# Where the low halves of the attention probabilities are formed, and four smaller edits to a hybrid attention and convolution block

## The chip, the cores and the metric

The kernel runs on one core of a Trainium2 chip. Its time is device microseconds of one execution. Three runs of the kernel before gave a median of 634.66 us, between 634.0 and 635.41. A profile is one more execution, recorded by the hardware profiler: this one took 634.12 us, of which 632.3 us lie between the first and the last recorded instruction (the span). The granted TensorE clock was 1.000 in it.

A core has five engines that work through their own instruction streams in order: TensorE (PE in the profile, with its weight loads as PEld), VectorE (DVE), ScalarE (ACT), GpSimd (POOL) and SyncE (SP), which here only issues transfers. They wait for each other through semaphores.

## The reference

One layer of a latent-diffusion backbone: modulated RMS norm, one wide projection, two-dimensional neighbourhood attention that shares its softmax with 256 context keys, a gated short convolution beside it, and an output projection (1024 tokens, width 1024, 8 heads of 64):

```python
h = rmsnorm(x, norm_g) * (1 + scale[:, None]) + shift[:, None]
hc = rmsnorm(ctx, norm_g) * (1 + scale_c) + shift_c
q, k, v, za, u, bg, cg, zc = jnp.split(h @ w_in, SPLIT_POINTS, axis=-1)
...
kc, vc = jnp.split(hc @ w_in[:, D_ATTN:3 * D_ATTN], 2, axis=-1)
...
s = jnp.concatenate([s_lat.reshape(*s_lat.shape[:4], n_lat), s_ctx], axis=-1)
p = jax.nn.softmax(s, axis=-1).astype(v.dtype)
...
attn = neighbourhood_attention(q, k, heads(v), kc, vc, rpb) * jax.nn.silu(za)
conv = gated_short_conv(u, bg, cg, zc, conv_w, conv_b)
x_new = x + gate[:, None] * (jnp.concatenate([attn, conv], axis=-1) @ w_out)
```

`scale` and `shift` come from `silu(c) @ w_ada`, a 1024 x 3072 matrix.

## The kernel before

**Split numbers.** Nearly every product is made of three float32r matmuls: an operand `a` is cast to a high half (`act.copy`, or the exponential itself, written as float32r), the low half is the difference between `a` and that high half (`tensor_tensor(lo, a, hi, subtract)`), and `mm3` adds high times high, high times low and low times high. So each weight or activation tile costs one cast and one difference before TensorE may use it.

**Stages.** (1) From 0 to about 77 us: the slabs of `w_ada`, 1024 x 256 pieces `slabs[m, j]` (m = 0 to 3, j = 0 for shift and 1 for scale), are multiplied by the condition vector (`products`, into the PSUM tile `tr`), `modulation` turns the rows into columns, `transposed` transposes a k-slice of the normed x on TensorE, `turn` applies scale and shift and makes high and low halves, and `first_columns` projects the first 384 columns of the convolution (`acc`). From slab (1, 1) on, slabs are split into halves by `split`, in two parts of four k-tiles (lines 609 to 616). (2) To about 265 us: q, k and v of all heads (`pacc`), norm, rotation, context keys (`cacc`), stored to DRAM. (3) To about 541 us: attention, with the other projections (`pu`) as filler on TensorE. (4) The output projection (`pout`).

**Order.** In stages 1 and 3 the list `strict` is filled: every engine executes its instructions in the order in which the code emits them. In stage 4 it is empty, and a planner orders the instructions of each engine.

**A quarter of the attention.** `quarter(n)` (line 1091) is called 36 times; head and group are `divmod(n, 4)`, a group being 256 of the 1024 queries of a head. Three groups are in work at a time: `n` has its scores made, `e = n - 2` its exponentials, `o = n - 3` its sums with v. In the order of the code:

- TensorE transposes the running maxima `mx` of group `e` into `pmx`; VectorE reduces them to the row maxima `rm` (line 1105).
- `ctx_out(o)`: TensorE multiplies the context exponentials `phc`, `plc` by the context values into `po`.
- `do_dves(3)`: VectorE does waiting chores (weight halves `ul`, convolution `cv`, `cu`, gating `zs`, `tb`), those of the slow queue at most three a quarter; `gating` has more.
- TensorE transposes `rm` back, ScalarE copies it to `mg`; then the latent scores of group `n` (`pss`), the context scores (`pc`, copied to `sc` by ScalarE).
- `ctx_exp(e)` (line 1047): VectorE subtracts `mg` from `sc`, ScalarE makes the exponential twice, as float32r `phc` and in place in `sc`, and GpSimd forms `plc = sc - phc` (line 1055).
- The same for the latent scores: `w` (a view of tile `sb`) minus the maxima, two exponentials, one into `phl`.
- one filler tick (six 512-column matmuls), then `lat_out(o)`: `phl`, `pll` times v.
- VectorE adds the bias to the scores of group `n` (`sb`), and takes maxima into `mx`: `ctx_max` (one operand in PSUM), `lat_max` for two key blocks (both operands in SBUF).
- VectorE forms `pll = w - phl` for group `e` (line 1160).
- the remaining filler ticks; `TICKS[n]` has their number for each quarter, 2 to 4.

Thus the next quarter's first transposes need the last `lat_max`, and its `rm` stands on VectorE behind `pll`.

**The output stage.** `load_wo(wp, nh, f)` loads a 128 x 512 tile of `w_out` into a raw buffer `woraw` through ScalarE's queue, multiplies it by the gate if `nh` is 1, and splits it into `woh` and `wol`; `put_y` does the same for an activation tile. `out_tile` adds the residual and stores. The last tile, (nh, t) = (1, 7), is made in two pieces of 256 columns, each accumulated in its own bank over 24 matmuls, so that the first piece's addition and store run while TensorE makes the second.

Of the kernel before, what the change touches and what calls it, by code (L numbers as in the profile page):

```python
# [10 lines left out]
F32 = mybir.dt.float32  # L11
# [28 lines left out]
def body(tc, es, x, ctxt, w_ada, b_ada, w_in, q_g, k_g, rpbr, w_out, vecs, cst, out):  # L40
# [565 lines left out]
    def norm(xtile, n):  # L606
        dve.tensor_scalar(xtile, xtile, sums[n], None, ALU.mult)

    def split(m, j, part, cast=act.copy):

        if part == 0:
            highs[j] = hcp.tile([P, KT, 256], F32R, name="slabh", tag="AB"[j])
            lows[j] = place(6 + j, [P, KT, 256], F32R, "slabl")
        rows = slice(4 * part, 4 * part + 4)
        cast(highs[j][:, rows], slabs[m, j][:, rows])
        dve.tensor_tensor(lows[j][:, rows], slabs[m, j][:, rows], highs[j][:, rows].bitcast(F32), ALU.subtract)

    def products(m, j, kts=range(KT), parts=(0, 1)):

        if m not in mods:  # L620
            mods[m] = tr()
        rows = mods[m][:4 if m else 2, 256 * j:256 * j + 256]
        split_ = [(c4, highs[j]), (c4, lows[j])] if (m, j) >= (1, 1) else [(c0 if m else c2, slabs[m, j])]
        for i, (c, part) in enumerate(split_):
            for kt in kts if i in parts else ():
                pe.matmul(rows, c[:, kt], part[:, kt], start=(i == 0 and kt == 0 and j == 0),
                          stop=(i == len(split_) - 1 and kt == KT - 1 and j == 1), skip_group_check=True)
# [46 lines left out]
    def transposed(half, k, ts=range(4)):  # L674
        if (half, k) not in pts:
            pts[half, k] = tr()
        for i in ts:
            pe.transpose(pts[half, k][:, i * P:(i + 1) * P], xx[4 * half + i][:, k * P:(k + 1) * P], ident)

    def turn(half, k, on, between=None):  # L680

        modulated(rows_of(hh[k], half), rows_of(hl[k], half),
                  pts.pop((half, k))[:].rearrange("p (r b c) -> p r b c", r=8, b=8), k, 0, on, between)
# [97 lines left out]
        norm(xx[t - 1], t - 1)  # L781
    first_columns(0, 1)
    norm(xx[7], 7)
    split(1, 1, 0)
    split(1, 1, 1, dve.tensor_copy)
    products(1, 0)
    transposed(1, 0)
    turn(1, 0, act)
    load_slab(2, 1)
    load_chunks([4, 5])  # L790
# [113 lines left out]
    def bank(name, tag):  # L904
        return (pss if tag == "S" else psm).tile([P, 512], F32, name=name, tag=tag, bufs=2)
# [60 lines left out]
    class head:  # L966
# [80 lines left out]
        def ctx_exp(self, g):  # L1047
            sc = self.cps[g]
            m = mg[:, g * 256:(g + 1) * 256].rearrange("p (o q) -> p o q", o=1)
            dve.tensor_tensor(sc, sc, m.broadcast_to([P, 2, 256]), ALU.subtract)  # L1050
            ph = ap.tile([P, 2, 256], F32R, name="phc", tag="phc", bufs=2)
            pl = ap.tile([P, 2, 256], F32R, name="plc", tag="plc", bufs=2)
            act.activation(ph, sc, AF.Exp)
            act.activation(sc, sc, AF.Exp)
            pool.tensor_tensor(pl, sc, ph[:].bitcast(F32), ALU.subtract)
            self.cps[g] = ph, pl

        def ctx_out(self, g):
            ph, pl = self.cps.pop(g)
# [31 lines left out]
    def quarter(n):  # L1091

        live = lambda m: 0 <= m < 4 * NH
        ticks = TICKS[n]
        e, o = n - 2, n - 3
        if live(e):
            hd, g = heads[e // 4], e % 4  # L1100
            pm = psm.tile([P, 512], F32, name="pmx", tag="C", bufs=2)
            for i in range(2):
                pe.transpose(pm[:, i * P:(i + 1) * P], mx[:, (2 * g + i) * P:(2 * g + i + 1) * P], ident)
            rm = ap.tile([P, 2], F32, name="rm", tag="rm", bufs=8)
            dve.tensor_reduce(rm, pm[:, :256].rearrange("p (i k) -> p i k", i=2), AX.X, ALU.max)
        if live(o):
            heads[o // 4].ctx_out(o % 4)
        do_dves(3)
        if gating and next(gating[0], "end"):
            gating.pop(0)  # L1110
        if live(e):
            for i in range(2):
                pe.transpose(pm[:, 256 + i * P:256 + (i + 1) * P], rm[:, i:i + 1].broadcast_to([P, P]), ident)
            act.copy(mg[:, g * 256:(g + 1) * 256], pm[:, 256:512])
        now = pair_of(n)
        for i, hd_, j in now:
            hd_.scores(j, sbank[:, i])
        if n == 0:
            next(fill)
            ticks -= 1  # L1120
        if live(n):
            heads[n // 4].ctx_scores(n % 4)
        if live(e):
            hd.ctx_exp(g)
        if e in sbs or e in exps:
            pair, sb = pair_of(e), sbs.pop(e)
            w = both(sb, e, pair)
            dve.tensor_tensor(w, w, maxima_of(e, pair), ALU.subtract)
            exps[e] = [ap.tile([P, 2, 384], F32R, name=m, tag=m, bufs=2) for m in ("phl", "pll")]
            ph, pl = (both(v, e, pair) for v in exps[e])  # L1130
            act.activation(ph, w, AF.Exp)
            act.activation(w, w, AF.Exp)
        for _ in range(n > 0):
            next(fill, None)
        done = []
        if o >= 0:
            pho, plo = exps.pop(o)
            for i, hd_, j in pair_of(o):
                hd_.lat_out(j, pho[:, i], plo[:, i])
                if j in (4, 7):  # L1140
                    done.append((hd_, j // 7))
                    if j == 7 and hd_.s:
                        ready.append(hd_.p)
        if now:
            sb = sbs[n] = sb_new()
            g_ = n % 4
            if g_:
                bt = now[0][1].bt
                bias = bt[:, 1:2].broadcast_to([P, 2, 384]) if g_ == 2 else bt[:, 0:2] if g_ == 1 else bt[:, 1:3]
                dve.tensor_tensor(sb, sbank[:, :, :384], bias, ALU.add)  # L1150
            else:
                for i, hd_, j in now:
                    cols = slice(P, 384) if j == 0 else slice(0, 256)
                    dve.tensor_tensor(sb[:, i, :256], sbank[:, i, :256], hd_.bt[:, 1, cols], ALU.add)
            if live(n):
                heads[n // 4].ctx_max(n % 4)
            for i, hd_, j in now:
                hd_.lat_max(j, sb[:, i])
        if e in sbs or e in exps:
            dve.tensor_tensor(pl, w, ph.bitcast(F32), ALU.subtract)  # L1160
        for _ in range(ticks - (n > 0)):
            next(fill, None)
        for hd_, bank_ in done:
            hd_.finish(bank_)
        do_acts()

    heads = [head(h) for h in range(NH)]
    sbs, exps, ready = {}, {}, []


    def fillers():
# [195 lines left out]
    y, wo = {}, {}  # L1367

    def load_wo(wp, nh, f):
        raw = op.tile([P, 512], F32, name="woraw", tag="woraw", bufs=2)  # L1370
        act.dma_start(raw, w_out[0, f * P:(f + 1) * P, nh * 512:(nh + 1) * 512])
        if nh:
            dve.tensor_tensor(raw, raw, gate[:, 512:], ALU.mult)
        wh = wp.tile([P, 512], F32R, name=f"woh{nh}{f}")
        wl = wp.tile([P, 512], F32R, name=f"wol{nh}{f}")
        act.copy(wh, raw)
        dve.tensor_tensor(wl, raw, wh[:].bitcast(F32), ALU.subtract)  # L1377
        wo[nh, f] = wh, wl
# [38 lines left out]
    def out_tile(ps, nh, t, pieces=(slice(0, 512),)):  # L1417
        rows, cols = slice(t * P, (t + 1) * P), slice(nh * 512, (nh + 1) * 512)
        xr = rp.tile([P, 512], F32, name="xr", tag="xr", bufs=3)
        sp.dma_start(xr, x[0, rows, cols])  # L1420
        ot = rp.tile([P, 512], F32, name="ot", tag="ot", bufs=3)
        if nh:
            for c in pieces:
                part = slice(c.start + 512, c.stop + 512)
                dve.tensor_tensor(ot[:, c], ps[c.start // 256][:, c], xr[:, c], ALU.add)
                sp.dma_start(out[0, rows, part], ot[:, c])
        else:
            dve.tensor_tensor(ot, ps, gate[:, cols], ALU.mult)
            pool.tensor_tensor(ot, ot, xr, ALU.add)
            sp.dma_start(out[0, rows, cols], ot)  # L1430
# [7 lines left out]
    for t in first:  # L1438
        out_tile(first[t], 0, t)
    for n, (nh, t) in enumerate([(0, 6), (0, 7)] + [(1, t) for t in range(NB)]):  # L1440
        pieces = [slice(0, 256), slice(256, 512)] if (nh, t) == (1, NB - 1) else [slice(0, 512)]
        ps = [bank("pout", "USC"[(n + i) % 2 + i]) for i in range(len(pieces))]
        for c, b in zip(pieces, ps):
            for f in FORDER:
                out_mm(b, nh, t, f, c)
        out_tile(ps if nh else ps[0], nh, t, pieces)


# [49 lines left out]
```

## Time and profile before

| | us |
|---|---|
| median of three runs | 634.66 |
| the profiled execution, whole | 634.12 |
| its span | 632.3 |
| ScalarE busy | 327.7 |
| VectorE busy | 447.7 |
| GpSimd busy | 121.4 |
| of which `plc`, 32 subtractions | 42.8 |
| last recorded matmul's start | 629.0 |

A line of the profile names the engine, the operation, the tiles (`out<-in`, buffer numbers left out), the shape of the result and of the input (partitions x elements), the count, and in a summary the busy time and the mean of one in ns. Most instructions of stages 1 to 3 carry the line of a helper, L55, so tiles identify them. In a list in order of time the columns are start and duration in us; a bracket tells how long the engine was idle before the instruction and what ended that. In a list of waits they are the total, the number and the longest. A matmul's recorded duration covers its way through the array, so consecutive matmuls overlap, and only the distances of their starts show the rate: a 512-column matmul is recorded with 0.39 us and followed by the next after 0.23. In a list of stretches the columns after the window are its length and the busy time of PE, PEld, DVE, ACT and POOL with instruction counts, then the clock and the transfers.

### The profile page before, as it was taken

The numbers are of one execution on the slowest core, as the hardware profiler recorded it, in microseconds if no ns is written. First come the engines' busy times: TensorE is split into PE (matmuls) and PEld (weight loads), VectorE is DVE, ScalarE is ACT, GpSimd is POOL, SyncE is SP. The second block draws the span as 40 slices with busy tenths as digits, with TensorE's granted clock in tenths as the row PEclk, the third lists the DMA queues.
The fourth block names the chain that finished last, engine by engine and source line by source line (L and its number), as shares of the span: only waits on it lengthen the run. The fifth ranks groups of instructions, "written<-read, shape, count | busy, mean of one in ns | idle before, by whom it ended". The sixth has DMA issues, their size and how long they took to land.

```text
span 632.3 us, 10096 instructions
## 1 busy us (share of the span) xinstructions
PE 624.3 (99%) x3503; PEld 538.8 (85%) x3504; DVE 447.7 (71%) x834; ACT 327.7 (52%) x705; POOL 121.4 (19%) x134
## 2 busy tenths in 40 slices
PE   8999999999999999999999999999999999999998
PEld 3577899999999999888888888888888888888887
DVE  1887858766856755478898889988998964477411
ACT  5676935424625446345576568567775854352000
POOL 1305014123223222001121111111111112003300
PEclk9999999999999999999999999999999999999999
DMA  8973648867775993975383736683842233965721
GB/s 319 381 268 106 179 116 258 263 195 213 265 245 169 293 337 134 330 221 194 103 286 100 237 104 209 190 277 101 269 131 75 59 103 123 316 204 183 237 101 50
DMA packets 103007, 125.61 MB, mean 199 GB/s; under 512 B 9665, under 2 KB 71577, under 8 KB 101676
## 3 DMA queue, kind: packets, MB, share of 16 engines
q1 hardware_dynamic: 96492, 113.38, 54.8%
q10 hardware_dynamic: 6208, 11.05, 5.6%
q0 software_dynamic: 256, 0.54, 0.4%
q8 instruction: 27, 0.44, 0.3%
q14 instruction: 24, 0.20, 0.1%
HBM read 88.09 MB, written 38.62 MB: 200 GB/s over the span
## 4 chain that ended last, share of the span: by engine, by line
PE 78%; DVE 7%; DMA 6%; issue 6%; ACT 1%; SPq 1%; POOL 1%; DVEq 0%; POOLq 0%; ACTq 0%
PE pu L55 24%; PE pacc L55 21%; PE po L55 7%; PE acc L55 5%; PE cacc L55 4%; PE tr L55 3%; PE pss L55 3%; PE pmx L55 2%; DVE mx L55 2%; PE pout L75 2%; PE pout L76 2%; PE pout L74 2%; PE pc L55 2%; DMA slab<-in_w_ada 2%; DVE sb L55 2%
## 5 line engine op out<-in xcount | busy, mean ns | idle before, releaser
L55 PE MATMUL pu<-h,uh 128*128 128x512 f32 x544 | 169.1, 392 | 0.0
L55 PE MATMUL pacc<-wh,h 128*128 128x384 f32 x512 | 135.1, 338 | 0.0
L55 PEld LDWEIGHTS pu<-h,uh 128*128 128x128 f32 x544 | 98.1, 188 | 17.0
L55 PE MATMUL pu<-h,ul 128*128 128x512 f32 x272 | 106.3, 391 | 0.0
L55 PEld LDWEIGHTS pacc<-wh,h 128*128 128x128 f32 x512 | 92.9, 188 | 0.1
L55 PE MATMUL pacc<-wl,h 128*128 128x384 f32 x256 | 85.6, 335 | 0.0
L55 POOL TENSOR_TENSOR plc<-sc,phc 128x512 fp32r<-128x512 f32 x32 | 42.8, 1339 | 215.9 <-ACT sc L55 159.2
L55 POOL TENSOR_TENSOR ss<-ss,few 128x4 f32<-128x4 f32 (+1 forms) x40 | 41.4, 1038 | 125.3 <-DVE ss L55 125.1
L55 PEld LDWEIGHTS pu<-h,ul 128*128 128x128 f32 x272 | 51.1, 188 | 11.2
L55 DVE TENSOR_TENSOR mx<-mx,sb 128x384 f32<-128x384 f32 (+1 forms) x64 | 59.1, 932 | 2.0
L75 PE MATMUL pout<-wol,yh 128*128 128x512 f32 (+1 forms) x136 | 51.3, 377 | 0.1
L76 PE MATMUL pout<-woh,yl 128*128 128x512 f32 (+1 forms) x136 | 50.7, 377 | 0.0
L74 PE MATMUL pout<-woh,yh 128*128 128x512 f32 (+1 forms) x136 | 49.7, 376 | 0.0
L55 PEld LDWEIGHTS pacc<-wl,h 128*128 128x128 f32 x256 | 48.1, 188 | 0.1
L55 DVE TENSOR_REDUCE ss<-sq 128x4 f32<-128x260 f32 (+1 forms) x40 | 15.7, 394 | 40.8 <-ACT sq L55 40.8
L55 ACT ACTIVATE sq<-pacc 128x256 f32<-128x256 f32 x32 | 12.3, 385 | 52.5 <-PE pacc L55 52.0
L55 ACT COPY mg<-pmx 128x256 f32<-128x256 f32 x32 | 11.9, 373 | 51.7 <-PE pmx L55 45.3
L55 ACT COPY sc<-pc 128x512 f32<-128x512 f32 x32 | 18.8, 589 | 25.8 <-PE pc L55 25.8
L55 ACT ACTIVATE qn<-pacc,ss 128x64 f32<-128x64 f32 x128 | 30.1, 330 | 3.0 <-issue 2.5
L55 DVE TENSOR_TENSOR pll<-sb,phl 128x768 fp32r<-128x768 f32 (+2 forms) x33 | 28.4, 861 | 4.5 <-ACT sb L55 4.5
L55 PE MATMUL po<-phl,v 128*65 128x256 f32 (+2 forms) x160 | 31.2, 291 | 0.0
L75 PEld LDWEIGHTS pout<-wol,yh 128*128 128x128 f32 x136 | 25.6, 188 | 5.2 <-DVE wol L1377 0.5
(163 smaller groups left out, 1266.0 us busy)
## 6 DMA issues: line engine op xcount, KB each, us to landing
uraw<-in_w_in SPq DMA_DIRECT2D x34, 256.0 KB
q_d<-qs SPq DMA_DIRECT2D x32, 256.0 KB
k_s<-k_d SPq DMA_DIRECT2D x8, 1024.0 KB
q_s<-q_d SPq DMA_DIRECT2D x16, 512.0 KB
wr<-in_w_in SPq DMA_DIRECT2D x40, 192.0 KB
slab<-in_w_ada SPq DMA_DIRECT2D x6, 1024.0 KB
v_d<-vs SPq DMA_DIRECT2D x20, 260.0 KB
v<-v_d SPq DMA_DIRECT2D x16, 325.0 KB
```

The source lines that it names most:

```text
L55: i = emit(*a, **kw)
L74: i = pe.matmul(ps, ah, bh, start=first, stop=False)
L75: pe.matmul(ps, ah, bl, start=False, stop=False)
L76: pe.matmul(ps, al, bh, start=False, stop=last)
```

## The change

Five edits in one:

- `ctx_exp` no longer emits the difference `plc`; it returns a function that emits it on VectorE, and `quarter` calls this after the maxima of group `n`.
- The latent difference `pll` is put off: it goes into the list `lat_rest` and is emitted in the next quarter, behind that quarter's `rm`. If the next quarter has two ticks, or there is none, it is emitted at its old place, which is now behind `plc`.
- For slab (1, 1), ScalarE casts the first part and VectorE the second before either difference; the other slabs keep the order cast, difference for each part. TensorE's transposes for `turn(1, 0)` go ahead of the last two k-tiles of `products(1, 0)`.
- The raw tiles of `w_out` get four buffers instead of two.
- The last output tile is cut into 384 and 128 columns, with the banks kept by a piece's first column.

```diff
@@ -606,14 +606,23 @@
     def norm(xtile, n):
         dve.tensor_scalar(xtile, xtile, sums[n], None, ALU.mult)
 
-    def split(m, j, part, cast=act.copy):
+    def cast_slab(m, j, part, cast):
 
         if part == 0:
             highs[j] = hcp.tile([P, KT, 256], F32R, name="slabh", tag="AB"[j])
             lows[j] = place(6 + j, [P, KT, 256], F32R, "slabl")
         rows = slice(4 * part, 4 * part + 4)
         cast(highs[j][:, rows], slabs[m, j][:, rows])
+
+    def rest_of(m, j, part):
+
+        rows = slice(4 * part, 4 * part + 4)
         dve.tensor_tensor(lows[j][:, rows], slabs[m, j][:, rows], highs[j][:, rows].bitcast(F32), ALU.subtract)
+
+    def split(m, j, part):
+
+        cast_slab(m, j, part, act.copy)
+        rest_of(m, j, part)
 
     def products(m, j, kts=range(KT), parts=(0, 1)):
 
@@ -781,10 +790,13 @@
         norm(xx[t - 1], t - 1)
     first_columns(0, 1)
     norm(xx[7], 7)
-    split(1, 1, 0)
-    split(1, 1, 1, dve.tensor_copy)
-    products(1, 0)
+    cast_slab(1, 1, 0, act.copy)
+    cast_slab(1, 1, 1, dve.tensor_copy)
+    rest_of(1, 1, 0)
+    rest_of(1, 1, 1)
+    products(1, 0, range(6))
     transposed(1, 0)
+    products(1, 0, range(6, KT))
     turn(1, 0, act)
     load_slab(2, 1)
     load_chunks([4, 5])
@@ -1052,8 +1064,8 @@
             pl = ap.tile([P, 2, 256], F32R, name="plc", tag="plc", bufs=2)
             act.activation(ph, sc, AF.Exp)
             act.activation(sc, sc, AF.Exp)
-            pool.tensor_tensor(pl, sc, ph[:].bitcast(F32), ALU.subtract)
             self.cps[g] = ph, pl
+            return lambda: dve.tensor_tensor(pl, sc, ph[:].bitcast(F32), ALU.subtract)
 
         def ctx_out(self, g):
             ph, pl = self.cps.pop(g)
@@ -1103,6 +1115,8 @@
                 pe.transpose(pm[:, i * P:(i + 1) * P], mx[:, (2 * g + i) * P:(2 * g + i + 1) * P], ident)
             rm = ap.tile([P, 2], F32, name="rm", tag="rm", bufs=8)
             dve.tensor_reduce(rm, pm[:, :256].rearrange("p (i k) -> p i k", i=2), AX.X, ALU.max)
+        while lat_rest:
+            lat_rest.pop()()
         if live(o):
             heads[o // 4].ctx_out(o % 4)
         do_dves(3)
@@ -1121,7 +1135,7 @@
         if live(n):
             heads[n // 4].ctx_scores(n % 4)
         if live(e):
-            hd.ctx_exp(g)
+            ctx_rest = hd.ctx_exp(g)
         if e in sbs or e in exps:
             pair, sb = pair_of(e), sbs.pop(e)
             w = both(sb, e, pair)
@@ -1156,8 +1170,12 @@
                 heads[n // 4].ctx_max(n % 4)
             for i, hd_, j in now:
                 hd_.lat_max(j, sb[:, i])
+        if live(e):
+            ctx_rest()
         if e in sbs or e in exps:
-            dve.tensor_tensor(pl, w, ph.bitcast(F32), ALU.subtract)
+            lat_rest.append(lambda: dve.tensor_tensor(pl, w, ph.bitcast(F32), ALU.subtract))
+            if n + 1 >= len(TICKS) or TICKS[n + 1] == 2:
+                lat_rest.pop()()
         for _ in range(ticks - (n > 0)):
             next(fill, None)
         for hd_, bank_ in done:
@@ -1165,7 +1183,7 @@
         do_acts()
 
     heads = [head(h) for h in range(NH)]
-    sbs, exps, ready = {}, {}, []
+    sbs, exps, ready, lat_rest = {}, {}, [], []
 
 
     def fillers():
@@ -1367,7 +1385,7 @@
     y, wo = {}, {}
 
     def load_wo(wp, nh, f):
-        raw = op.tile([P, 512], F32, name="woraw", tag="woraw", bufs=2)
+        raw = op.tile([P, 512], F32, name="woraw", tag="woraw", bufs=4)
         act.dma_start(raw, w_out[0, f * P:(f + 1) * P, nh * 512:(nh + 1) * 512])
         if nh:
             dve.tensor_tensor(raw, raw, gate[:, 512:], ALU.mult)
@@ -1422,7 +1440,7 @@
         if nh:
             for c in pieces:
                 part = slice(c.start + 512, c.stop + 512)
-                dve.tensor_tensor(ot[:, c], ps[c.start // 256][:, c], xr[:, c], ALU.add)
+                dve.tensor_tensor(ot[:, c], ps[c.start][:, c], xr[:, c], ALU.add)
                 sp.dma_start(out[0, rows, part], ot[:, c])
         else:
             dve.tensor_tensor(ot, ps, gate[:, cols], ALU.mult)
@@ -1438,11 +1456,11 @@
     for t in first:
         out_tile(first[t], 0, t)
     for n, (nh, t) in enumerate([(0, 6), (0, 7)] + [(1, t) for t in range(NB)]):
-        pieces = [slice(0, 256), slice(256, 512)] if (nh, t) == (1, NB - 1) else [slice(0, 512)]
-        ps = [bank("pout", "USC"[(n + i) % 2 + i]) for i in range(len(pieces))]
-        for c, b in zip(pieces, ps):
+        pieces = [slice(0, 384), slice(384, 512)] if (nh, t) == (1, NB - 1) else [slice(0, 512)]
+        ps = {c.start: bank("pout", "USC"[(n + i) % 2 + i]) for i, c in enumerate(pieces)}
+        for c in pieces:
             for f in FORDER:
-                out_mm(b, nh, t, f, c)
+                out_mm(ps[c.start], nh, t, f, c)
         out_tile(ps if nh else ps[0], nh, t, pieces)
```

## The prediction, made before the result was known

> **What bounds the kernel now.** I read the busy table first, then what TensorE waits for, then the order of single instructions where it waits.
>
> ```profile
> span 632.3 us, 10096 instructions
> PE 624.3 (99%) x3503; PEld 538.8 (85%) x3504; DVE 447.7 (71%) x834; ACT 327.7 (52%) x705; POOL 121.4 (19%) x134
> ```
>
> ```profile
> PE pmx L55 <- DVE rm L55: 1.0, 4, 0.5
> PE pmx L55 <- DVE mx L55: 0.7, 3, 0.3
> ```
>
> TensorE is the bound, and a change off TensorE can only win the time in which it stands still. The second fence (waits from 255 us to 632 us) shows only 1.7 us in seven waits, but that is short: a matmul's record lasts longer than the distance to the next start, and the overlap swallows the beginning of each wait. Starts tell more (TensorE, in order of time):
>
> ```profile
> 283.74 0.28 PE L55 MATMUL po<-plc,v 128*65 128x256 f32 x1
> 283.86 0.41 PE L55 MATMUL pmx<-ci,rm 128*128 128x128 f32 x2
> ...
> 303.29 0.39 PE L55 MATMUL pu<-h,ul 128*128 128x512 f32 x1
> 303.72 0.30 PE L55 MATMUL pmx<-ci,mx 128*128 128x128 f32 x1
> 304.22 0.33 PE L55 MATMUL pmx<-ci,mx 128*128 128x128 f32 x1 [0.20 <-DVE mx L55]
> ...
> 304.62 0.28 PE L55 MATMUL po<-plc,v 128*65 128x256 f32 x1
> ...
> 304.98 0.28 PE L55 MATMUL po<-plc,v 128*65 128x256 f32 x1
> 305.43 0.43 PE L55 MATMUL pmx<-ci,rm 128*128 128x128 f32 x2 [0.17 <-DVE rm L55]
> ```
>
> From the last `plc` product to the `rm` transpose takes 0.12 us undisturbed (283.74 to 283.86) and 0.45 here: 0.33 lost where the list shows 0.17, so 0.16 is hidden per wait. Seven waits are worth 1.7 + 7 x 0.16 = 2.8 us. Shorter ones are not listed at all, like the 0.43 from 303.29 to 303.72, where a 512-column matmul's usual distance is 0.23: 0.2 lost. I estimate five of these, 0.9 us: 3.7 in all. The longest, 0.52 + 0.16 at 277.37, comes ahead of the first `plc`, which is made later in that quarter, and stays:
>
> ```profile
> 277.37 0.43 PE L55 MATMUL pmx<-ci,rm 128*128 128x128 f32 x2 [0.52 <-DVE rm L55]
> ```
>
> So about 3.0 us of the attention stage can be won, and each piece waits for the row maxima on VectorE.
>
> **Why the maxima are late.** GpSimd, then VectorE, one quarter:
>
> ```profile
> 287.39 1.31 POOL L55 TENSOR_TENSOR plc<-sc,phc 128x512 fp32r<-128x512 f32 x1 [5.17 <-ACT sc L55]
> ```
>
> ```profile
> 287.50 1.61 DVE L55 TENSOR_TENSOR mx<-mx,sb 128x384 f32<-128x384 f32 x1
> 289.14 0.56 DVE L55 TENSOR_TENSOR mx<-mx,sb 128x384 f32<-128x384 f32 x1
> ```
>
> The same maximum takes 1.61 us while GpSimd's `plc` subtraction runs and 0.56 when it doesn't; the long one ends 0.41 us after GpSimd does (289.11 against 288.70). It is held, not slowed. By form, 270 to 530 us:
>
> ```profile
> L55 DVE TENSOR_TENSOR mx<-mx,sb 128x384 f32<-128x384 f32 x48 | 46.6, 972 | 1.6
> ...
> L55 DVE TENSOR_TENSOR pll<-sb,phl 128x768 fp32r<-128x768 f32 x24 | 22.8, 950 | 3.5 <-ACT sb L55 3.5
> L55 DVE TENSOR_TENSOR sc<-sc,mg 128x512 f32<-128x512 f32 x32 | 21.9, 684 | 10.1 <-ACT mg L55 10.1
> ...
> L55 DVE TENSOR_TENSOR mx<-pc,sc 128x256 f32<-128x256 f32 x32 | 13.3, 415 | 1.0 <-ACT sc L55 0.9
> L55 DVE TENSOR_TENSOR mx<-mx,sb 128x256 f32<-128x256 f32 x16 | 12.5, 813 | 0.3
> ```
>
> **The change, part by part.**
>
> *Context subtraction to VectorE.* It removes 32 GpSimd instructions and adds 32 on VectorE. The trace has none there; the nearest row is `sc<-sc,mg`, same size and two operands in SBUF: 0.684 us, 21.9 us in all. Released, the maxima would take 48 x 0.56 + 16 x 0.415 = 33.5 us instead of 46.6 + 12.5 = 59.1: 25.6 us saved. VectorE comes out 3.7 us lighter; more to the point, the last maximum of a quarter ends up to 1 us earlier, and 0.68 stands ahead of the next `rm` where 0.95 stood. The new wait is TensorE's for `plc`: the first product that needs it starts 0.40 us after the second transpose (304.22 to 304.62), 0.5 after the first, and VectorE is done with `plc` 0.7 us after the last maximum, so a quarter is free of this wait once its maxima end 0.2 us ahead of TensorE.
>
> *Latent subtraction behind the next `rm`.* It puts 0.95 us ahead of the next quarter's work. Where VectorE waits for ScalarE's `mg` (10.1 us over 32 quarters) this fills the gap and costs nothing; where chores fill that gap already, it pushes the maxima of that quarter back by up to 0.87 (0.95 less overlap). The heavy quarter before 472 us shows the risk:
>
> ```profile
> 468.94 0.42 DVE L55 TENSOR_TENSOR mx<-pc,sc 128x256 f32<-128x256 f32 x1
> 469.39 1.67 DVE L55 TENSOR_TENSOR mx<-mx,sb 128x384 f32<-128x384 f32 x2
> 470.98 0.95 DVE L55 TENSOR_TENSOR pll<-sb,phl 128x768 fp32r<-128x768 f32 x1
> 471.85 0.42 DVE L55 TENSOR_REDUCE rm<-pmx 128x2 f32<-128x256 f32 x1
> ```
>
> Here the two maxima take 1.67 together, 0.5 above their free time; with 0.6 to 0.87 put in front they end no earlier, and this quarter wins about 0.1 of its 0.34. Queued behind the moved instruction are the chores, and behind those ScalarE's exponentials, needed a quarter later. I take off 0.1 more and book the attention stage at **-2.9**, between -1.5 (only what the list shows, less the first wait and a little) and -4.0.
>
> *Split slab.* Four waits in a row, VectorE then TensorE:
>
> ```profile
> 26.07 0.75 DVE L55 TENSOR_SCALAR xx<-xx,xss 128x1024 f32<-128x1024 f32 x1 [0.44 <-POOL xss L55]
> 27.22 1.23 DVE L55 TENSOR_TENSOR slabl<-slab,slabh 128x1024 fp32r<-128x1024 f32 x1 [0.39 <-ACT slabh L55]
> 28.36 0.69 DVE L55 CAST slabh<-slab 128x1024 fp32r<-128x1024 f32 x1
> ```
>
> ```profile
> 28.06 0.72 PE L55 MATMUL tr<-slabh,c 128*4 128x256 f32 x4
> 29.10 0.63 PE L55 MATMUL tr<-slabh,c 128*4 128x256 f32 x4 [0.31 <-DVE slabh L55]
> ...
> 30.03 0.60 PE L55 MATMUL tr<-ci,xx 128*128 128x128 f32 x4
> ```
>
> The cast goes to 26.8, into VectorE's 0.39 us gap, and ends at 27.5. TensorE, four matmuls of 0.12 from 28.06, then goes on at 28.54 instead of 29.10: 0.56. The differences end at 28.6 and 29.8, before their products. Drawing four transposes (4 x 0.11) ahead of two products leaves TensorE's work as it was, lets ScalarE's `h` start sooner, and delays by 0.44 us the load on SyncE's queue that waits for slab (1, 0), with the chunk loads behind it. TensorE's list for the whole run has one wait for a slab, the one at 29.10, so later slabs have slack:
>
> ```profile
> PE tr L55 <- DVE slabh L55: 0.3, 1, 0.3
> ```
>
> I book **-0.55** (-0.2 to -0.8).
>
> *Four raw buffers.* With two, each load waits for the difference two tiles back, ScalarE standing behind it:
>
> ```profile
> 589.07 1.02 DVE wol L1377
> ...
> 590.14 0.50 PE pout L75
> ```
>
> The last difference for the second half of `w_out` is ready at 590.1, when TensorE needs it; the first matmul behind it lasts 0.50 against an even 0.23, so 0.27 goes. TensorE arrives 3.5 us sooner after the change, but so does all that sets this chain off. With loads two ahead the chain shortens by more: **-0.3** (-0.4 to +0.6, if TensorE's earlier arrival is not matched).
>
> *Last tile cut at 384 instead of 256.* This is TensorE work at the very end, hidden by nothing.
>
> ```profile
> 77.00 12.50 PE pacc L55 x72
> ```
>
> ```profile
> 629.04 0.12 PE pout L75
> ...
> 629.32 0.42 DVE ot L1425
> ```
>
> Before: 48 x 0.12 = 5.76. After: 24 matmuls of 384 columns at 12.50/72 = 0.174, and 24 of 128. No row has 128 columns against 128-column float32r weights. Half of 0.12, 0.06, is the low end; the high end is the transposes of 128 columns against 128 x 128 weights, (0.60 - 0.27)/3 = 0.11, taking 0.27 as one record. The weight-load rows say which is nearer:
>
> ```profile
> L55 PEld LDWEIGHTS acc<-h,wh 128*128 128x128 f32 x28 | 4.9, 188 | 1.8 <-DVE h L55 0.7 <-ACT h L55 0.2
> ...
> L55 PEld LDWEIGHTS tr<-slabh,c 128*4 128x4 f32 x14 | 1.1, 85 | 0.9 <-DVE slabh L55 0.6
> ```
>
> 124 more columns cost 103 ns, so loading 128 takes about 0.107, longer than a 128-column product streams. I take 0.109: 4.17 + 2.62 = 6.79, +1.03. The last add shrinks from 0.42 to about 0.28 (0.27 less per 256 columns, by the 684 and 415 rows): -0.14. The last transfer is halved; I book nothing. **+0.9** (-0.4 to +1.1).
>
> The Trainium skill's "TensorE: Matmul & The Clock Gate", section "LDWEIGHTS (loading the stationary operand)", has a load cost its columns over 1.2 in ns, 107 for 128, which speaks against this edit as the rows do. Its section "Back-to-back issue gap" gives 81 ns sustained at 128 columns instead; by that the edit would cost, as an estimate from that page, 4.17 + 1.94 - 5.76 - 0.14 = +0.2, and the sum would be 0.7 lower.
>
> **The sum** against the profiled execution: 634.12 - 2.9 - 0.55 - 0.3 + 0.9 = 631.3. That execution lies 0.5 below the median of the runs, inside their spread of 634.0 to 635.4, so I leave the figure at **631.3**.
>
> **Rivals.** *The moved subtraction eats the release* (0.15). If in every quarter with chores the maxima gain nothing and ScalarE's exponentials drift late with them, only quarters with an open `mg` gap win, about half: attention -1.3, total 632.9. For it: VectorE was busy 83.84 of 90 us between 380 and 470; against it: its idle time sits in that gap.
>
> ```profile
> 380.00:470.00 90.00, 89.95 (x518) 76.72 (x517) 83.84 (x127) 64.41 (x103) 16.00 (x14) 1.00 0.60 194
> ```
>
> *VectorE becomes the bound* (0.08), the slower side. If the long maxima are not GpSimd's doing, none of the 25.6 us returns and each quarter gains 0.68 on VectorE. In that stretch twelve quarters of 7.5 us add 8.2 to 83.8: 92 in 90, 2 us late before any wait, and the same in the similar stretch from 470 on; with the present 3.0 kept and the other parts at their values, 634.12 + 4 + 0.05 = 638. It decides once a maximum shortens by less than the 0.68 added. Against it stands the end of the long maximum 0.41 after GpSimd's.
>
> *The gain is met again* (0.12): the first latency-bound waits or the output stage's chain take the 2.9 back, and head and tail cancel; 634.
>
> **How the numbers follow.** Forecast 0.65 (629.5 to 632.5), rivals 0.15, 0.08, 0.12. Changes under 0.2%, 1.3 us, can't be told from none. Faster by more takes the forecast and most of the first rival: 0.79; same 0.13; slower 0.08. The range runs from 629.5 to 633.9, which leaves out the slower rival, part of the last and the forecast's thin low end.
>
> **What would show it.** No `mx<-mx,sb` above 0.6 us in the attention stage and a mean near 0.52; `plc` on VectorE near 0.68 us, GpSimd busy near 79 us, VectorE near 444; TensorE's waits for `rm` and `mx` down to the one near 277; an unbroken run of `slabh` products; even `pout` distances near 590; 24 last products about 0.11 us apart. The forecast is wrong if maxima stay above 1 us, if new waits for `plc` or `pll` stand on TensorE, or if the last 128 columns run at 0.06.

## The result, and the profile after

The changed kernel takes 632.8 us in the median of 13 runs (632.31 to 633.51), the kernel before 635.24 us in its 13 (633.61 to 636.52). The ratio is 0.9965, with a 95% interval from 0.9957 to 0.9973: about 2.2 us less. Its profiled execution took 632.67 us.

The busy table and the chain that ended last, of the changed kernel:

```profile
span 630.9 us, 10022 instructions
...
PE 624.0 (99%) x3504; PEld 540.3 (86%) x3504; DVE 436.8 (69%) x866; ACT 327.7 (52%) x705; POOL 77.6 (12%) x102
...
PE 96%; DMA 1%; DVE 1%; SPq 1%; issue 0%; ACT 0%; ACTq 0%
```

VectorE took over 32 subtractions and still lost 11 us of busy time; the chain runs over TensorE for 96% of the span, beside 78% before.

The starts of TensorE's first and last matmuls of each stage divide the two profiled executions, 634.12 and 632.67 us, like this:

| stretch | before | after | difference |
|---|---|---|---|
| start to first `pss` | 267.63 | 267.32 | -0.31 |
| first `pss` to last `po` (attention) | 258.65 | 257.08 | -1.57 |
| last `po` to first `pout` | 15.08 | 15.08 | 0.00 |
| first `pout` to the last tile's first piece | 81.99 | 81.60 | -0.39 |
| last tile's two pieces, to the last start | 5.63 | 6.70 | +1.07 |
| last matmul's start to the end of the span | 3.35 | 3.10 | -0.25 |
| sum | | | -1.45 |

Three runs below have the same attention as the changed kernel. They took 256.81, 256.96 and 256.98 us for it, so one trace tells this stretch to about 0.3 us.

VectorE's instructions by form between 270 and 530 us, changed kernel:

```profile
L55 DVE TENSOR_TENSOR mx<-mx,sb 128x384 f32<-128x384 f32 x48 | 26.8, 558 | 1.6
...
L55 DVE TENSOR_TENSOR plc<-sc,phc 128x512 fp32r<-128x512 f32 x32 | 21.9, 685 | 0.5 <-ACT sc L55 0.5
L55 DVE TENSOR_TENSOR sc<-sc,mg 128x512 f32<-128x512 f32 x32 | 21.9, 683 | 1.5 <-ACT mg L55 1.1
...
L55 DVE TENSOR_TENSOR mx<-mx,sb 128x256 f32<-128x256 f32 x16 | 6.2, 423 | 0.3
```

The maxima fell from 46.6 + 12.5 to 26.8 + 6.2 us, and no single one is above 0.57. The new subtraction costs 0.685 us, and the wait for `mg` shrank from 10.1 to 1.1 us in 32 quarters, because `pll` now stands in that gap. TensorE's waits from 255 to 632 us:

```profile
PE pu L55 <- DVE cv L55: 0.6, 2, 0.5
PE pmx L55 <- DVE rm L55: 0.5, 1, 0.5
```

Of the seven waits for maxima and row maxima one is left, that of the first quarter with `rm`, as forecast. Two waits of another kind are new. TensorE and VectorE at the longer one:

```profile
480.32 0.40 PE L55 MATMUL pc<-q_s,kc_s 128*128 128x256 f32 x2
481.17 0.73 PE L55 MATMUL pu<-h,uh 128*128 128x512 f32 x2 [0.45 <-DVE cv L55]
481.74 0.40 PE L55 MATMUL pu<-h,ul 128*128 128x512 f32 x1
```

```profile
478.62 0.42 DVE L55 TENSOR_REDUCE rm<-pmx 128x2 f32<-128x256 f32 x1 [1.82 <-PE pmx L55]
478.96 0.95 DVE L55 TENSOR_TENSOR pll<-sb,phl 128x768 fp32r<-128x768 f32 x1
479.83 0.68 DVE L55 TENSOR_TENSOR ul<-uraw,uh 128x512 fp32r<-128x512 f32 x1
480.43 1.28 DVE L55 TENSOR_TENSOR cv<-pu,cv 128x512 f32<-128x512 f32 x2
```

`cv<-pu` reads a filled PSUM tile of the filler, and the filler's next matmuls go into that tile. The first of the two chores ends at 480.43 + 0.68 = 481.11; `pu` starts at 481.17. Without the 0.87 us of `pll` (0.95 less the overlap with the next record) in front, the tile would have been free at 480.24, before TensorE came for it. The second place, at 403.53 us, is the same chore one convolution group earlier.

Below, a late start is the distance of a matmul's start from the one before it, less what the same two kinds of matmul usually have between them.

### The profile page after: what moved, and what is told of

It reads as the page before. It is cut to its first block, busy times and chain, and to the rows that moved or that the text cites. A ratio compares the mean times of both kernels' runs of the same rounds, so it can differ in the third digit from the quotient of the medians.

```text
span 630.9 us, 10022 instructions
## 1 busy us (share of the span) xinstructions
PE 624.0 (99%) x3504; PEld 540.3 (86%) x3504; DVE 436.8 (69%) x866; ACT 327.7 (52%) x705; POOL 77.6 (12%) x102
## 4 chain that ended last, share of the span: by engine, by line
PE 96%; DMA 1%; DVE 1%; SPq 1%; issue 0%; ACT 0%; ACTq 0%
PE pu L55 30%; PE pacc L55 21%; PE po L55 8%; PE acc L55 5%; PE pout L76 5%; PE pout L75 5%; PE pout L74 5%; PE cacc L55 4%; PE tr L55 4%; PE pss L55 3%; PE pmx L55 2%; PE pc L55 2%; DMA xx<-in_x 1%; PE trA L55 1%; PE trB L55 1%
## 5 line engine op out<-in xcount | busy, mean ns | idle before, releaser
L75 PE MATMUL pout<-wol,yh 128*128 128x512 f32 (+2 forms) x136 | 51.6, 379 | 0.0
L74 PE MATMUL pout<-woh,yh 128*128 128x512 f32 (+2 forms) x136 | 50.5, 379 | 0.0
L76 PE MATMUL pout<-woh,yl 128*128 128x512 f32 (+2 forms) x136 | 49.8, 379 | 0.0
L55 DVE TENSOR_REDUCE rm<-pmx 128x2 f32<-128x256 f32 x32 | 13.6, 424 | 30.4 <-PE pmx L55 30.2
L55 DVE TENSOR_TENSOR mx<-mx,sb 128x384 f32<-128x384 f32 (+1 forms) x64 | 33.0, 524 | 2.0
```

What stands on the lines that cost most here:

```text
L55: i = emit(*a, **kw)
L74: i = pe.matmul(ps, ah, bh, start=first, stop=False)
L75: pe.matmul(ps, ah, bl, start=False, stop=False)
L76: pe.matmul(ps, al, bh, start=False, stop=last)
```

## The experiments

Two theories are told apart by the first two runs. Theory 1: GpSimd's subtraction holds the maxima, and its move is what wins; the put-off of `pll` is a help that only pays with it. Theory 2: what wins is that `rm` no longer stands behind `pll`.

### The context subtraction alone

The kernel before, with the first edit only:

```diff
-            pool.tensor_tensor(pl, sc, ph[:].bitcast(F32), ALU.subtract)
             self.cps[g] = ph, pl
+            return lambda: dve.tensor_tensor(pl, sc, ph[:].bitcast(F32), ALU.subtract)
...
-            hd.ctx_exp(g)
+            ctx_rest = hd.ctx_exp(g)
...
+        if live(e):
+            ctx_rest()
         if e in sbs or e in exps:
             dve.tensor_tensor(pl, w, ph.bitcast(F32), ALU.subtract)
```

> The kernel before with one edit: the context difference plc on VectorE behind the maxima, the latent difference pll left at its old place (now behind plc, ahead of the next rm). Theory 1 (GpSimd's subtraction holds the maxima): no maximum over 0.6 us, TensorE's waits for mx gone, waits for rm partly left because rm now stands behind 0.6 + 0.87 us, no wait of pu for cv; attention (first pss to last po) 1.5 to 3 us shorter than the 258.7 of before, time 0.25 to 0.45% less. Theory 2 (the gain is rm's freedom from pll): VectorE has 0.6 us more ahead of each rm and nothing is won, attention the same or up to 3 us longer.

Measured: 634.22 us beside 635.24, ratio 0.9989 (0.9978 to 1.0); attention 257.72 us, 0.93 shorter. Its maxima by form and its waits of TensorE from 255 to 530 us, then VectorE in the quarter that lost most before:

```profile
L55 DVE TENSOR_TENSOR mx<-mx,sb 128x384 f32<-128x384 f32 x48 | 26.8, 558 | 1.7
```

```profile
PE pmx L55 <- DVE rm L55: 2.0, 5, 0.5
```

```profile
302.53 1.15 DVE L55 TENSOR_TENSOR mx<-mx,sb 128x384 f32<-128x384 f32 x2
303.60 0.69 DVE L55 TENSOR_TENSOR plc<-sc,phc 128x512 fp32r<-128x512 f32 x1
304.20 0.95 DVE L55 TENSOR_TENSOR pll<-sb,phl 128x768 fp32r<-128x768 f32 x1
305.07 0.42 DVE L55 TENSOR_REDUCE rm<-pmx 128x2 f32<-128x256 f32 x1
```

The long maxima are gone once the subtraction leaves GpSimd, and this run changes nothing else: the hold is shown. The trace of before tells its form. In it 30 maxima start while a `plc` subtraction runs, and each ends 0.41 to 0.42 us (384 columns) or 0.28 to 0.29 us (256 columns) after that subtraction, however early it began. That is 0.14 us less than the 0.56 and 0.42 that one takes alone, so it waited and then ran at its usual speed. The Trainium skill's "SBUF — State Buffer", section "Who interferes with whom", states it as a lock: VectorE with two SBUF inputs and a GpSimd instruction that reads SBUF exclude each other, the later one waiting until the other is through. This case agrees, with up to 1.61 us before and at most 0.57 here. The waits for `mx` are gone too, but those for `rm` grew, because 0.6 + 0.87 us now stand ahead of it. The gain is smaller than theory 1 had it. By the whole time, whose interval reaches 1.0, it could be nothing, as theory 2 had it; the attention stage, 0.93 us shorter, says that it is not.

### The put-off alone

The kernel before, with `pll` put off as in the change and `plc` left on GpSimd:

```diff
+        while lat_rest:
+            lat_rest.pop()()
...
-            dve.tensor_tensor(pl, w, ph.bitcast(F32), ALU.subtract)
+            lat_rest.append(lambda: dve.tensor_tensor(pl, w, ph.bitcast(F32), ALU.subtract))
+            if n + 1 >= len(TICKS) or TICKS[n + 1] == 2:
+                lat_rest.pop()()
```

> The kernel before with one edit: pll put off behind the next rm, plc left on GpSimd. Theory 1: maxima of 1.1 to 1.6 us stay, and in quarters full of chores they end up to 0.87 us later; attention 1 to 4 us longer than the 258.7 of before, time 0.2 to 0.6% more. Theory 2: rm follows the maxima at once, the waits for rm go, attention 1.5 us or more shorter.

Measured: 636.65 us, ratio 1.0031 (1.002 to 1.0043); attention 260.95 us, 2.3 longer. Maxima by form, then TensorE's waits from 255 to 530 us:

```profile
L55 DVE TENSOR_TENSOR mx<-mx,sb 128x384 f32<-128x384 f32 x48 | 45.1, 939 | 1.7
```

```profile
PE pmx L55 <- DVE mx L55: 1.6, 7, 0.3
PE pu L55 <- DVE cv L55: 0.7, 2, 0.5
PE pmx L55 <- DVE rm L55: 0.5, 1, 0.5
PE pmx L55 <- ACT uh L55: 0.4, 1, 0.4
```

Theory 2 falls. With the hold in place the put-off pushes the maxima back, seven listed waits for `mx` instead of three, and it brings the waits for `cv` by itself. (The list puts one more wait of `pmx`, 0.4 us, down to ScalarE's `uh`.) Of the two edits the first takes 0.9 us from the attention, the second adds 2.3, and both together take 1.6: the put-off is worth 0.6 us only where the maxima are free.

### The latent difference behind all chores

The changed kernel with the two lines of `lat_rest` moved down:

```diff
-        while lat_rest:
-            lat_rest.pop()()
         if live(o):
             heads[o // 4].ctx_out(o % 4)
         do_dves(3)
         if gating and next(gating[0], "end"):
             gating.pop(0)
+        while lat_rest:
+            lat_rest.pop()()
```

> The changed kernel with pll emitted behind the quarter's chores instead of ahead of them. If the chores that read PSUM tiles (cv<-pu) are what the deferred pll delays, TensorE's waits of pu for cv (0.34 and 0.61 us late starts in the changed kernel) go and attention is 1.0 to 1.4 us shorter than its 257.1, time about 631.6 beside a before of 635.2 (ratio 0.994 to 0.995). Rival: pll comes too late for its own products, waits of po for pll take the place, attention stays at 257.1 or above.

Measured: 634.7 us, ratio 0.9996 (0.9986 to 1.0006); attention 259.03 us. The rival won. TensorE's waits from 255 to 530 us, and the longest of them on VectorE and TensorE:

```profile
PE po L55 <- DVE pll L55: 2.2, 4, 0.8
PE pmx L55 <- DVE rm L55: 0.5, 1, 0.5
```

```profile
464.14 0.68 DVE L55 TENSOR_TENSOR zs<-zs,rb 128x512 f32<-128x512 f32 x1
464.86 0.69 DVE L55 TENSOR_TENSOR tb<-tb,zs 128x512 f32<-128x512 f32 x1
465.47 0.68 DVE L55 TENSOR_TENSOR pll<-sb,phl 128x512 fp32r<-128x512 f32 x1
```

```profile
466.21 0.33 PE L55 MATMUL po<-pll,v 128*65 128x256 f32 x1 [0.82 <-DVE pll L55]
```

The waits for `cv` are gone, so the chore's place was their cause, but `pll` behind five chores is too late for its own products: 2.98 us of late starts at five places took the place of the 1.2 us won.

### The last tile cut in halves again

```diff
-        pieces = [slice(0, 384), slice(384, 512)] if (nh, t) == (1, NB - 1) else [slice(0, 512)]
+        pieces = [slice(0, 256), slice(256, 512)] if (nh, t) == (1, NB - 1) else [slice(0, 512)]
```

> The changed kernel with the last tile cut 256 and 256 again. If 128-column products are bound by their weight load (0.11 us each), the last two pieces take 5.7 instead of 6.7 us on TensorE, the add 0.13 and the store 0.1 us more: 0.8 us less time than the changed kernel, ratio to before 0.995. Rival: the smaller last store is worth what the products cost, ratio 0.9965 as the changed kernel.

Measured: 632.27 us, ratio 0.9956 (0.9943 to 0.997). From the first `pout` to the last 87.23 us instead of 88.30, from the last to the end 3.34 instead of 3.10: 0.83 lost by the new cut in the traces. The times alone, 632.27 and 632.8 on different runs of before, would not tell it with certainty; the two stretches do. The 128-column products in the changed kernel and the add behind them, then products of its attention with as many columns but only 65 columns of weights (`128*65`):

```profile
625.34 0.27 PE L75 MATMUL pout<-wol,yh 128*128 128x128 f32 x1
625.45 0.27 PE L76 MATMUL pout<-woh,yl 128*128 128x128 f32 x1
625.56 0.28 PE L74 MATMUL pout<-woh,yh 128*128 128x128 f32 x1
...
628.10 0.29 DVE L1443 TENSOR_TENSOR ot<-pout,xr 128x128 f32<-128x128 f32 x1 [2.07 <-PE pout L76]
```

```profile
300.86 0.28 PE L55 MATMUL po<-phl,v 128*65 128x128 f32 x2
300.98 0.22 PE L55 MATMUL po<-pll,v 128*65 128x128 f32 x1
301.04 0.28 PE L55 MATMUL po<-phl,v 128*65 128x128 f32 x2
```

Starts in the last tile are 0.11 us apart, almost the 0.12 of twice as many columns. In the attention they are 0.06 apart with 65 columns of weights. So 128-column products have no shortest distance of 0.11 of their own; the load of 128 weight columns sets the pace. The Trainium skill's "TensorE: Matmul & The Clock Gate", section "LDWEIGHTS (loading the stationary operand)", has a load take its columns over 1.2 in ns, by which an estimate for 128 columns is 107 ns; the trace agrees. The 81 ns of the Trainium skill's section "Back-to-back issue gap" on that page does not hold for these float32r products: 0.11 was measured.

### Two raw buffers

```diff
-        raw = op.tile([P, 512], F32, name="woraw", tag="woraw", bufs=4)
+        raw = op.tile([P, 512], F32, name="woraw", tag="woraw", bufs=2)
```

> The changed kernel with two raw buffers. If the second half of w_out bounds the output stage with two buffers, a late start of 0.3 to 0.5 us stands in pout (first to last pout 88.6 to 88.8 us, 88.30 in the changed kernel), ratio 0.997. Rival: the late start of before was chance, as the two runs without it (the context edit alone, the deferral alone, both with two buffers) suggest: 88.30 us, ratio 0.9965.

Measured: 633.23 us, ratio 0.9975 (0.9962 to 0.9988); first to last `pout` 88.30 us, exactly as with four. The two runs with the attention edits alone have two buffers as well, and 87.23 us each, no late start. So of four traces with two buffers only the first, before the change, shows the 0.37 us at 590; the six other traces have four buffers and none. The times of two and of four buffers do not tell them apart either (0.9965 with four, the intervals overlap). The four buffers remove a chance event at most; how often it comes was not tried.

What they buy is room. With two buffers the last difference for the second half of `w_out` ended 0.21 us too late in the trace of before, and 0.35, 0.50 and 1.15 us ahead of its product in the other three traces; with four it ends 15 to 17 us ahead. A second hold belongs to this. GpSimd, then VectorE, in the trace of before:

```profile
584.03 1.29 POOL L1429 TENSOR_TENSOR ot<-ot,xr 128x512 f32<-128x512 f32 x1 [2.96 <-DMA xr<-in_x]
```

```profile
584.04 1.82 DVE L1377 TENSOR_TENSOR wol<-woraw,woh 128x512 fp32r<-128x512 f32 x1
```

Six differences and gate products of `w_out` are held like this there, to 1.01 to 1.82 us for 0.69, and end 0.55 us after GpSimd's addition. In the traces with four buffers they are all done before GpSimd's first addition, and none is held.

### Slab products undivided

```diff
-    products(1, 0, range(6))
-    transposed(1, 0)
-    products(1, 0, range(6, KT))
+    products(1, 0)
+    transposed(1, 0)
```

> The changed kernel with products(1, 0) undivided and its transposes behind it, as before, the casts still ahead of the differences. If the way there and back between slab products and transposes costs TensorE 0.19 us each, the first acc matmul behind the slab starts 6.2 us after the first of products(1, 0), beside 6.50 in the changed kernel. Rival: the transposes' place buys ScalarE's h its earlier start, and without it TensorE waits: 6.5 or more.

Measured once: 633.29 us; 6.71 us from the first slab product to the first `acc` matmul behind the slab, beside 6.50. TensorE in the changed kernel, then ScalarE, TensorE and VectorE in the run:

```profile
24.12 2.75 PE L55 MATMUL tr<-slab,c 128*4 128x256 f32 x12
26.81 0.66 PE L55 MATMUL tr<-ci,xx 128*128 128x128 f32 x4
27.39 1.03 PE L55 MATMUL tr<-slab,c 128*4 128x256 f32 x4
28.35 1.08 PE L55 MATMUL tr<-slabh,c 128*4 128x256 f32 x8
...
30.62 0.63 PE L55 MATMUL acc<-h,wh 128*128 128x512 f32 x2
```

```profile
28.89 0.78 ACT L55 ACTIVATE h<-tr,ab 128x512 fp32r<-128x512 f32 x1 [0.61 <-PE tr L55]
29.57 0.77 ACT L55 ACTIVATE hw<-tr,ab 128x512 f32<-128x512 f32 x1
```

```profile
29.65 0.64 PE L55 MATMUL tr<-slabl,c 128*4 128x256 f32 x4
30.39 0.66 PE L55 MATMUL tr<-ci,xx 128*128 128x128 f32 x4
30.80 0.72 PE L55 MATMUL tr<-slabl,c 128*4 128x256 f32 x4
```

```profile
28.32 2.36 DVE L55 TENSOR_TENSOR slabl<-slab,slabh 128x1024 fp32r<-128x1024 f32 x2 [0.36 <-ACT slabh L55]
```

The division does cost TensorE time, 0.09 us at each of its two added turns: the slab product at 27.39 starts 0.20 us behind the last transpose, where transposes are 0.11 apart, and the first `slabh` product at 28.35 starts 0.31 us behind the last slab product, where slab products are 0.22 apart. From the first slab product to the second `slabh` product all six traces with the division take 4.35 us and all four without it 4.16: 0.19 in all, and not twice 0.19 as the expectation had it. Without the division ScalarE's two instructions end at 30.34 and the next transposes start at 30.39, 0.26 late behind the products before them. The slab is not the cause. Its cast comes 2.59 us behind the first slab product, in the changed kernel 2.53; its second difference ended at 30.68, and the products that read it follow the transposes at 30.80 without a wait. ScalarE's pair starts only when the undivided products and the transposes behind them are through. So the forecast of 6.2 fails and the rival took place: the transposes' place buys ScalarE's earlier start, and the wait for ScalarE costs more than the two turns. The rest of the 0.21, about 0.14, lies in slightly longer distances between the later products and transposes.

All traces together say what the split is worth. With the old order the first `acc` matmul starts 4.79 to 4.80 us behind the first cast in all three traces (before, and the two with one attention edit), whatever the time of the slab; with the new order and the division it starts 6.50 us behind the first slab product in all six, while the cast comes 1.9 to 2.5 us behind that product. By the new rule the three old ones would have started 0.32, 0.83 and 0.81 us sooner. From that matmul to the first `pss` all ten traces take 236.6 to 236.7 us, so what is won there reaches the attention whole.

### Two versions with a better place for the latent difference

Both have the halves at the end. The first puts `pll` behind the chores in quarters 19 and 29 only:

```diff
-        while lat_rest:
+        while lat_rest and n not in (19, 29):
             lat_rest.pop()()
         if live(o):
             heads[o // 4].ctx_out(o % 4)
         do_dves(3)
+        while lat_rest:
+            lat_rest.pop()()
```

> The changed kernel with the last tile cut 256 and 256, and with pll behind the chores in the two quarters alone (19 and 29) in which TensorE waited for cv. If the place of pll must be chosen quarter by quarter, the late starts of pu behind cv (0.45 and 0.71 us with their echoes) go and no wait of po for pll comes: attention 255.7 to 256.1 us beside 257.1 in the changed kernel, ratio to before 0.993 to 0.994. Rival: pll is late in these two quarters too, attention 256.8 or more, ratio that of the run with the tail alone, 0.9956.

Measured: 631.05 us, ratio 0.9939 (0.9926 to 0.9951); attention 256.09 us. TensorE's waits from 255 to 632 us are down to one row:

```profile
PE pmx L55 <- DVE rm L55: 0.5, 1, 0.5
```

The second has it behind the three chores and ahead of the gating products in every quarter, by leaving out the first `while`.

> As the run before, but with one rule for all quarters: pll behind the three chores and ahead of the two gating products. If the five late pll of the run with pll behind everything were late because of the gating products, three of them go (0.88, 0.98 and 0.63 us) and 0.33 and 0.17 stay: attention 256.2 to 256.8 us, ratio 0.9945. Rival: the chores alone make pll late, attention stays near 259, ratio 0.997 to 0.999.

Measured: 631.83 us, ratio 0.9951 (0.9938 to 0.9963); attention 256.86 us. As expected, two late `pll` stayed (0.31 and 0.17 us) and those behind the gating products went; the attention lies 0.06 above the forecast of 256.2 to 256.8. The version by quarters is the fastest of all; its interval lies below that of the changed kernel (0.9957 to 0.9973). Beside the run with the halves alone the intervals overlap, and the attention tells them apart: 256.09 us for 256.81.

## Why the prediction was right, and where it was not

- **What bounds, and why the maxima were late**: right. The run with the first edit alone shows the hold.
- **Context subtraction**: right in its terms: 0.684 us forecast, 0.685 measured; maxima 33.5 forecast, 33.0 measured. VectorE came out at 436.8 us instead of 444. Of these 7.2 us, 2.9 are a larger overlap of neighbouring records, which 32 additions at full length ignore, 0.5 the maxima, and 3.8 the products and differences of `w_out` that GpSimd no longer holds.
- **Latent subtraction behind `rm`**: the step that failed in size. The prediction named the chores as queued behind the moved instruction, "and behind those ScalarE's exponentials, needed a quarter later", and left out that a chore which reads a PSUM tile releases it to TensorE's filler. Late starts over 0.095 us between 262 and 528 us fell from 4.06 to 2.56 us. The 3.4 us behind maxima and `rm` went, all but 0.12, as booked; 1.41 us of `pu` behind chores came, and 0.34 of `po` behind `plc`. So -1.57 in place of -2.9. Of the 1.41, about 1.2 stand behind `cv`; the other 0.25, at 385 us, wait for ScalarE's `zs<-pu` and stay in the version by quarters. The condition for `plc`, maxima 0.2 us ahead of TensorE, was right: it failed in two quarters. New waits for `plc` were one of the signs that the prediction named for being wrong; they came, but as late starts of 0.15 and 0.20 us that the list of waits does not show.
- **The quarter before 472 us**: forecast to win 0.1 of 0.34; its maxima stayed late by 0.12 and the next `plc` by 0.2, together what was lost before. It won nothing.
- **Split slab**: right in direction, -0.31 in the profiled pair for -0.55. The term missed is the 0.19 us that the two added turns between slab products and transposes cost. The wait itself was smaller than booked: the `slabh` product at 29.10 started 0.60 us behind the one before it in place of 0.12, so 0.48 and not 0.56 was to be won, since the first two of these products are 0.20 apart. How much it wins hangs on when the slab comes, up to 0.8 us.
- **Four raw buffers**: -0.39 for -0.3 in the profiled pair, but the wait that it removed is one that other traces with two buffers don't have. The late difference was real; that the size came out is luck. The forecast also set a record's length, 0.50, against a distance of starts, 0.23; by starts the matmul at 590.14 was 0.26 late and the next one 0.11.
- **Last tile**: right: +1.07 on TensorE for +1.03, and -0.25 for -0.14 behind it, since the halved store was booked at nothing and brought 0.1.
- **The rivals**: none took place as told. In size the result is the first rival's, the moved subtraction eating a part of the release: 632.8 beside its 632.9, attention -1.57 beside its -1.3, and outside the 629.5 to 632.5 that the forecast took for itself. The range held because it took most of that rival in. Its mechanism did not come, though: it has only about half of the quarters win, and of the 3.4 us behind maxima and `rm` all but 0.12 went.

The sum of the pair is -1.45 for -2.85; the medians differ by 2.4. The runs of before spread over 2.9 us and those after over 1.2. That the slab's arrival, which the new order no longer follows, makes part of the old spread would fit the numbers above, but was not shown.

## What to carry to other kernels

When an instruction is put ahead of others on an engine, list what each of the delayed ones releases, not only what it computes: a chore with no deadline of its own still had one, because TensorE's next accumulation needed its PSUM tile. GpSimd's subtraction cost VectorE more (26.1 us of held maxima) than the same subtraction costs on VectorE itself (21.9), so work moved to the busier of the two made it less busy; look for instructions whose recorded time jumps beside GpSimd's. And a last tile should not be cut below the column count at which the weights' load takes as long as the product.

## What was not expected of the hardware

The hold is complete, and short of it there is no slowing. A held instruction ends a fixed time after GpSimd's, 0.28, 0.41 or 0.55 us for 256, 384 or 512 columns, which is 0.14 less than its length alone. With GpSimd's subtraction away, 48 maxima of 384 columns have a mean of 558 ns. `mx<-pc,sc`, which reads PSUM and SBUF, kept its 415 ns mean under both, and the 21 of them that overlap a `plc` in the trace of before took 0.41 to 0.42 us. A profile shows the hold as a longer record and not as a wait. And the weights' load shows plainly in the last tile, 128 columns at 0.11 us against 256 at 0.12, and against 0.06 where only 65 columns of weights are loaded.
